# A copy between two DRAM arrays in eight walks: two DMA queues held apart in one address bit at a time

## The chip, the core and the metric

The kernel runs on one core of a Trainium2 chip. The core has 16 DMA engines, and this kernel uses nothing else for its work. The metric is the time of one execution on the device in microseconds. It was 812.63 us before the change (median of three runs, 812.08 to 813.83).

## The reference

```python
def setup_inputs():
    return {
        "x": np.random.randn(8192, 8192).astype(np.float32),
    }

def reference(x: np.ndarray) -> np.ndarray:
    return np.fft.ifftshift(x)
```

For even sizes, ifftshift swaps the halves in both directions: row r of the output is row (r + 4096) mod 8192 of the input, and within a row the two halves of 4,096 columns change places. Nothing is computed. 268.44 MB are read and 268.44 MB written.

## The kernel before

Input and output are arrays in DRAM, and every DMA copies from the one straight into the other. A row of 8,192 floats is 32 KB, a half row 16 KB. A DMA covers half rows only, since the two halves of a row go to different places: `h` is 0 or `hc` (4,096 columns), the half that is written, and the other half of the source row is read.

The helper `copy` (line 26) issues one DMA on a queue. Its access pattern has three dimensions. The first, of 16, steps by one row and is what the 16 DMA engines share out, so each engine gets one row of 16 neighbouring ones. The second, of `per` = 16, steps by 16 rows, so it moves all engines on by 512 KB of addresses (a block of 16 rows). The third is the half row, one contiguous run of 16 KB and one DMA packet. A DMA thus has 256 half rows, 4 MB.

The loop at line 36 takes 1,024 rows at a time, four DMAs of 256 rows for each of two queues: SP's (`nc.sync`, q1) and ACT's (`nc.scalar`, q10). SP's queue writes left halves (`h` = 0) of row groups 0, 1, 2, 3; ACT's queue writes right halves of row groups 2, 3, 0, 1. So the two queues are 512 rows, 16 MB, apart, and in opposite halves, as long as they run side by side. There are 32 DMAs on each queue.

The order in a queue is that of the program. The framework gives each queue four semaphores in turn, so a DMA is issued once the fourth DMA before it in the same queue has landed; up to four are in flight in each. Nothing else orders the work, and no two DMAs touch the same output.

Of the kernel before, what the change touches and what calls it, by code (L numbers as in the profile page):

```python
# [1 line left out]

# [4 lines left out]


ENGINES = 16


@with_exitstack
def kernel(
    ctx: ExitStack,
    tc: tile.TileContext,
    x: bass.AP,
    out: bass.AP,
):
    nc = tc.nc
    R, C = x.shape  # L20
    hr = R // 2
    hc = C // 2
    per = 16
    rows = ENGINES * per

    def copy(queue, row, h, step):

        dims = [[C, ENGINES], [step * C, per], [1, hc]]
        queue.dma_start(
            out=bass.AP(out.tensor, out.offset + row * C + h, dims),  # L30
            in_=bass.AP(x.tensor, x.offset + (row + hr) % R * C + hc - h, dims),
        )

    for first in range(0, R, 4 * rows):
        for n in range(4):
            copy(nc.sync, first + n * rows, 0, ENGINES)
            copy(nc.scalar, first + (n + 2) % 4 * rows, hc, ENGINES)


# [1 line left out]
_INS = ['x']  # L43
_OUTS = [((8192, 8192), 'float32')]


def kernel(**inputs):
    import numpy as _np
    import concourse.bacc as _bacc
    import concourse.tile as _tile  # L50
    from concourse import mybir as _mybir
    from concourse.bass_utils import run_bass_kernel_spmd as _run

    nc = _bacc.Bacc("TRN2", target_bir_lowering=False, num_devices=1)  # L54
    arrays, args = {}, []
    for name in _INS:
        a = _np.ascontiguousarray(inputs[name])
        if a.dtype.kind in "iu":
            a = a.astype(_np.int64)
        arrays[f"in_{name}_dram"] = a  # L60
        args.append(nc.dram_tensor(f"in_{name}_dram", a.shape, _mybir.dt.from_np(a.dtype), kind="ExternalInput").ap())
    for i, (shape, dtype) in enumerate(_OUTS):
        dt = _mybir.dt.from_np(_np.dtype(dtype))
        args.append(nc.dram_tensor(f"out_{i}_dram", shape, dt, kind="ExternalOutput").ap())
    with _tile.TileContext(nc) as tc:
        kernel(tc, *args)
    r = _run(nc, [arrays], core_ids=[0])
    got = tuple(r.results[0][f"out_{i}_dram"] for i in range(len(_OUTS)))
    return got[0]
```

## Time and profile before

| | |
|---|---|
| time, median of 3 runs | 812.63 us (812.08 to 813.83) |
| profiled execution, span | 812.4 us |
| read and written | 268.44 MB each, 661 GB/s together over the span |
| DMA packets | 17,408, of which 1,024 are under 512 B (the completions) |
| issues | 32 on SP's queue, 32 on ACT's, 4,096 KB each, 101.0 us to landing (median) |
| duration of an issue | 571 ns (SP, median), 578 ns (ACT, median) |

The profiled execution lies 0.2 us under the median of the three runs. The profile gives, for each of the two queues, how many packets it had, how many MB they moved, and the time that the packets took as a share of what 16 engines have in the span. The row of DMA digits shows the same share in 40 slices of the span. Compute engines have no work here, and the chain that ended last names none of the copying, since DMA engines are not among its steps; so the queues, the waits of the issuing engines and the single packets are what there is to read. q1 is SP's queue and q10 ACT's.

### The profile page before, as it was taken

To read this page: it belongs to the slowest core of one execution; us is meant where nothing else is said; L and a number is where in the kernel's file an instruction comes from. 1 tells how busy PE (TensorE), PEld (TensorE's weight loads), DVE (VectorE), ACT (ScalarE), POOL (GpSimd) and SP (SyncE) were. 2 spreads that over 40 slices of the span, in tenths; PEclk is the share of its full clock that TensorE was granted. 3 is DMA by queue.
4 is the path that set the end of the run, shared out by engine and by line. 5 is a ranking of instruction groups with operands and counts; after the bars stand their busy time and mean duration, and the time that the engine had idled before them with its cause. 6 is when DMAs were issued, how large, how long until landed. Compare 5 with 4: busy or idle time off the path is not lost. (4 is left out here: it accounts for less than half of the span.)

```text
span 812.4 us, 109 instructions
## 1 busy us (share of the span) xinstructions
POOL 0.2 (0%) x4
## 2 busy tenths in 40 slices
POOL 0000000000000000000000000000000000000000
DMA  9999999999999999999999999999999999999998
GB/s 307 331 331 336 335 331 331 335 325 337 334 332 336 331 333 332 334 339 332 332 334 331 329 331 334 332 328 333 330 334 335 334 328 333 332 331 330 338 331 280
DMA packets 17408, 268.44 MB, mean 330 GB/s; under 512 B 1024, under 2 KB 1024, under 8 KB 1024
## 3 DMA queue, kind: packets, MB, share of 16 engines
q1 hardware_dynamic: 8704, 134.22, 49.7%
q10 hardware_dynamic: 8704, 134.22, 49.5%
HBM read 268.44 MB, written 268.44 MB: 661 GB/s over the span
## 5 line engine op out<-in xcount | busy, mean ns | idle before, releaser
L54 POOL MEMSET const-bfloat16-1.0<- 128x1 bf16 x1 | 0.1, 101 | 0.0
L54 POOL MEMSET const-uint8-127<- 128x1 uint8 x1 | 0.1, 101 | 0.0
L54 POOL MEMSET const-float32-0.0<- 128x1 f32 x1 | 0.1, 98 | 0.2 <-issue 0.2
L54 POOL MEMSET const-float32-1.0<- 128x1 f32 x1 | 0.1, 98 | 0.0
## 6 DMA issues: line engine op xcount, KB each, us to landing
out_dram<-in_x_dram SPq DMA_DIRECT2D x32, 4096.0 KB, 101.0
out_dram<-in_x_dram ACTq DMA_DIRECT2D x32, 4096.0 KB, 101.0
```

Of the source, the lines that this page charges most:

```text
L54: nc = _bacc.Bacc("TRN2", target_bir_lowering=False, num_devices=1)
```

## The change

The rows are divided into eight walks of 1,024 rows (64 blocks of 16 rows). In each walk both queues still copy every half row once between them, one packet for each, over the same 16 engines. What differs is which block each queue is at.

- Walk 0: SP writes blocks 0 to 31, ACT blocks 32 to 63, in opposite halves; then the halves change over. DMAs of 16 blocks, as before.
- Walks 1 to 5 (`apart` with bit 1, 2, 4, 8, 16): SP takes only blocks whose number has that bit clear, ACT only those with the bit set. As a block is 512 KB, the bit is 512 KB, 1 MB, 2 MB, 4 MB or 8 MB of the address. Both queues write the same half, first left, then right. A DMA steps by twice the bit, and so has 32, 16, 8, 4 or 2 blocks.
- Walk 6: bit 1 (512 KB) again, with the queues in opposite halves.
- Walk 7: SP takes blocks 0 to 31 and ACT 32 to 63, in steps of 8 blocks, four to a DMA; the queues are 16 MB apart and alike in all five bits, and in the same half.

There are 84 DMAs on each queue. The waits keep their form: each for the fourth DMA before it in its queue.

```diff
-    per = 16
-    rows = ENGINES * per
 
-    def copy(queue, row, h, step):
-
-        dims = [[C, ENGINES], [step * C, per], [1, hc]]
+    def copy(queue, row, h, by, steps):
+        dims = [[C, ENGINES], [by * ENGINES * C, steps], [1, hc]]
+        dst = out.offset + row * C + h
+        src = x.offset + (row + hr) % R * C + hc - h
         queue.dma_start(
-            out=bass.AP(out.tensor, out.offset + row * C + h, dims),
-            in_=bass.AP(x.tensor, x.offset + (row + hr) % R * C + hc - h, dims),
+            out=bass.AP(out.tensor, dst, dims),
+            in_=bass.AP(x.tensor, src, dims),
         )
 
+    part = 64
 
+    def walk(base, sync, scalar, by, steps, halves):
 
-    for first in range(0, R, 4 * rows):
-        for n in range(4):
-            copy(nc.sync, first + n * rows, 0, ENGINES)
-            copy(nc.scalar, first + (n + 2) % 4 * rows, hc, ENGINES)
+        for hs, ha in halves:
+            for a, b in zip(sync, scalar):
+                copy(nc.sync, (base + a) * ENGINES, hs, by, steps)
+                copy(nc.scalar, (base + b) * ENGINES, ha, by, steps)
+
+    like = ((0, 0), (hc, hc))
+    unlike = ((0, hc), (hc, 0))
+
+    def apart(base, bit, halves):
+        walk(base, range(bit), range(bit, 2 * bit), 2 * bit, part // (2 * bit), halves)
+
+    walk(0, (0, 16), (32, 48), 1, 16, unlike)
+    apart(1 * part, 1, like)
+    apart(2 * part, 2, like)
+    apart(3 * part, 4, like)
+    apart(4 * part, 8, like)
+    apart(5 * part, 16, like)
+    apart(6 * part, 1, unlike)
+    walk(7 * part, range(8), range(32, 40), 8, 4, like)
```

## The prediction

> **What bounds the kernel now.** I read the page first: its DMA row, its queue part and its issue part. Then I asked for the waits of the issuing engines, and last for the queue table of short windows.
>
> ```profile
> span 812.4 us, 109 instructions
> DMA  9999999999999999999999999999999999999998
> GB/s 307 331 331 336 335 331 331 335 325 337 334 332 336 331 333 332 334 339 332 332 334 331 329 331 334 332 328 333 330 334 335 334 328 333 332 331 330 338 331 280
> ...
> q1 hardware_dynamic: 8704, 134.22, 49.7%
> q10 hardware_dynamic: 8704, 134.22, 49.5%
> ...
> out_dram<-in_x_dram SPq DMA_DIRECT2D x32, 4096.0 KB, 101.0
> out_dram<-in_x_dram ACTq DMA_DIRECT2D x32, 4096.0 KB, 101.0
> ```
>
> The 16 DMA engines are busy from end to end; the two queues together fill 99.2% of them. No engine computes anything. Each queue has 8,192 packets of 16 KB and 512 small completion packets of 9 ns (32 DMAs on 16 engines). So one engine carries 1,024 large packets, and 0.992 x 812.4 / 1,024 = 787 ns is the mean of one. The packet records say that a quarter and more of them take exactly 611 ns and one in ten over 1,055 ns: 611 ns is the engine's own pace, the other 176 ns are memory. Packets of one engine follow without a gap, q1 and q10 in turn.
>
> The waits of the queues show that issuing is no bound:
>
> ```profile
> SPq L29 <- DMA out_dram<-in_x_dram: 689.4, 28, 25.3
> SPq L65 <- DMA out_dram<-in_x_dram: 102.2, 2, 79.5
> ```
>
> A DMA waits for the landing of the fourth before it in its own queue; three more are queued on the engines meanwhile, so these 689.4 us cost nothing.
>
> Two neighbouring windows of the queue table (packets, MB, share of 16 engines) show what does vary:
>
> ```profile
> q1 hardware_dynamic: 65, 1.06, 55.6%
> q10 hardware_dynamic: 67, 1.10, 47.9%
> ```
>
> ```profile
> q10 hardware_dynamic: 67, 1.10, 56.7%
> q1 hardware_dynamic: 61, 0.90, 40.9%
> ```
>
> These are 239.3 to 245.5 us and 245.5 to 251.7 us. In the first, a packet of q1 took 0.556 x 16 x 6,200 / 65 = 849 ns and one of q10 709; in the second q1's 55 large packets (0.90 MB) took 738 and q10's 839. Call 16 rows, 512 KB of addresses, a block; each queue is at one block at a time, ACT's queue about 3.3 blocks behind SP's. Summing all packet records by their own block: with the block's 2 MB bit clear 836 ns (q1) and 819 (q10), with it set 740 and 753. So an address bit of a packet's own moves its time by 80 ns. A packet reads and writes at the same offset in the two arrays (but for the half and 128 MB), so this looks like its reads meeting its neighbours' writes; that is my reading, not shown.
>
> **The change part by part.**
>
> *The same bytes, the same packets.* Every half row is still one 16 KB packet, every block is walked once per half, 16 consecutive rows lie on the 16 engines. What a packet's own 2 MB bit costs is therefore paid equally often: 0.
>
> *More DMAs.* 168 instead of 64 (4 + 4, 2 + 2, 4 + 4, 8 + 8, 16 + 16, 32 + 32, 2 + 2, 16 + 16), so 104 more completion packets per engine at 9 ns: +0.9 us on the path. Packets at a DMA's start are not longer than elsewhere (q1 850 ns at block 0 of a DMA, 843 at block 8; q10 787 and 809): 0 besides. Issuing rises from 32 to 84 per queue at 0.571 us (SP) or 0.578 us (ACT), 48 us in all beside 800. The cover is thinnest in the fifth single-bit walk, with DMAs of two blocks. Each new DMA there waits for the fourth before it on its own queue, and all later issues of that queue stand behind it; the other queue is not held. A block of a queue takes 2 x 787 = 1.574 us, so three DMAs of two blocks in flight give 9.4 us. Needed are 1.43 us from issue to first packet (0.73 us to 2.16 at the start), 0.35 us from a last packet to its landing, and the spread of the engines, at most 2.76 us between the first and last of 16 landings of one DMA: 4.5 us. Covered. Were the cover gone in both queues, 32 rounds of up to 4.5 us would cost 144 us.
>
> The Trainium skill ("DMA: Bandwidth & Descriptors", Measured) asks for at least 1 MiB a DMA for 75% of peak, with some 2 us fixed for each; the 512 KB ones break that. Paid once per pair of DMAs it would be 32 x 2 = 64 us, an estimate from that page; the landing rows above, with four in flight, speak against it.
>
> *The distance of the queues.* Before, they are 16 MB apart, less the lag of 3.3 blocks, so lower bits differ or not as the addition carries. I split the packet records by whether the block of the other queue differs in a bit: 512 KB 794 ns (alike 779), 1 MB 789 (786), 2 MB 787 (789), 4 MB 794 (782), 8 MB 796 (785), 16 MB 786 (796). Walking the two lists of blocks with the lag kept gives the share of time apart in each bit, before and after: 0.70 to 0.66, 0.35 to 0.57, 0.83 to 0.50, 0.41 to 0.62, 0.20 to 0.53, 0.90 to 0.58. Products: -0.6, +0.7, +0.7, +2.5, +3.6, +3.2 ns. The last three come largely from the same carries; I count the largest alone: -0.6 + 0.7 + 0.7 + 3.6 = 4.4 ns, x 1,024 = +4.5 us. All counted it is +10 us, none 0. The rows differ by 1 to 3 of their standard errors, so this is weak, but it is all the trace has.
>
> *Like halves, six walks of eight.* Before, the queues are in opposite halves throughout; no row shows the rest. Nearest: moments when over 80% of the running packets belong to one queue, so that nearly all read one half and write the other. These take 774 ns (q1) and 791 (q10), against 791 in even mixtures: like is not worse, and at best 8 ns better, -6 us over 768 packets. Far ends: every like packet in the fast or the slow class of the 2 MB bit, 747 or 828 ns against 787, which is 768 x -40 = -31 us or +31 us. I take 0, being nearest to the mixture rows.
>
> *Strides inside a queue.* An engine's next block is now 1 to 16 MB on, so neighbouring engines, 1 to 2 blocks out of step, are that far apart. It can meet or miss the same reads and writes; bounds as for the halves; I take 0, as each stride meets both classes.
>
> Sum: 812.4 + 0.9 + 4.5 = 817.8 us for the profiled execution; the median of the three runs, 812.63, lies 0.2 higher: **818.0 us**.
>
> **The rivals.**
>
> *Faster: reads and writes kept out of each other's way.* If the 80 ns of the 2 MB bit is a conflict of reads with writes, queues held in like halves keep all reads of both queues in one half. If half of the like packets reach the fast class: 0.5 x 768 x -40 = -15 us, 798 us. For it: the single-queue moments at 774. Against: q10's at 791. It decides once the halves give over 6 ns a packet.
>
> *No change.* Rows 16 apart sit on the same engine, which runs one packet at a time, so the queues never touch the same row position, and their distance does not matter. Only the 0.9 us remain: 813.5 us. For it: differences by bit no larger than 15 ns.
>
> *Slower by the halves.* The opposite: all reads in one half crowd it; half of the like packets in the slow class, +15 us beside the sum: 833 us; all of them, 849.
>
> *Starved queues.* If the engines spread over 9 us in the two-block walk, it costs a few us for each of 32 rounds, 3 x 32: about 910 us. Against: 2.76 us.
>
> *Lock-stepped strides.* If packets 4 to 16 MB apart alias, the walks of the 4 MB and 8 MB bits and the last one (304 us) run at the slowest tenth's 1,055 ns instead of 787: +104 us, 922 us. Against: 16 neighbouring rows are always in flight, 32 KB apart. The Trainium skill ("DMA: Bandwidth & Descriptors", Latency and other measured facts) reports this for copies of 16 KiB rows, 207 GB/s at a pitch of 512 KiB, 164 at 2 MiB, 103 at 4 and 8 MiB; the pitch between engines, which it speaks of, stays 32 KB here, and the queues' 16 MB already run at 330.
>
> **How the numbers follow.** Runs of this kernel tell 0.2% (1.6 us) from no change. Forecast (a little slower, 814.3 to 826) 0.37; slower by the halves 0.15; starved or aliased 0.06; no change 0.13; faster 0.29. Slower 0.58, same 0.13, faster 0.29. The range is to hold 8 in 10: it leaves out the starved and aliased cases, the outer part of the faster case below 798 and of the slower one above 838. The forecast's own range is 814 to 826.
>
> **What would show it.** Eight windows of some 101 us: the first should keep 332 GB/s, the two-block walk should show DMA at 9 throughout, and its issues should land within 13 to 15 us. A walk off by over 3% points to halves (if all like walks go together) or to one bit (if one walk stands out; the seventh, opposite, against the second, like, is the clean pair). Holes in the DMA row of the two-block walk would mean starving. I am wrong if like halves matter as much as the 2 MB bit does.

## The result and the profile after

The changed kernel took 814.69 us (median of 15 runs, 812.76 to 816.6) where the kernel before took 812.08 us (median of 15 runs beside it). The medians lie 2.6 us apart; the ratio worked out from all the runs is 1.0039, with a 95% interval of 1.0026 to 1.0051: slower by about 3.2 us (2.1 to 4.1). The forecast was 818.0 us.

The profiled execution spans 814.2 us, against 812.4 before. A time is not a span: this execution's time was 815.98 us, 1.8 above its span, and every execution with both figures shows 1.7 to 1.8. By that (an estimate) the execution profiled before was one of some 814.2 us, 1.6 above the median rather than 0.2 under it, so the two profiles show 1.8 of the 3.2 us. The page after, in the lines that answer to those shown of before:

```profile
span 814.2 us, 213 instructions
DMA  9999999999999999999999999999999999999998
GB/s 303 332 334 327 335 333 334 334 325 333 332 328 328 325 324 334 331 332 330 328 335 338 332 332 331 332 332 331 338 332 331 341 330 337 335 330 329 323 340 276
...
q1 hardware_dynamic: 9536, 134.22, 50.2%
q10 hardware_dynamic: 9536, 134.22, 48.9%
...
out_dram<-in_x_dram ACTq DMA_DIRECT2D x8, 4096.0 KB, 101.2
out_dram<-in_x_dram SPq DMA_DIRECT2D x8, 4096.0 KB, 103.2
```

The DMA engines are still full from end to end (50.2 + 48.9 = 99.1%), with 1,344 completion packets per queue instead of 512. In the packet records the mean large packet is 786.5 ns in both profiles; the 1.8 us between the spans are 0.9 us of completion packets per engine and 0.9 us more of idle time (7.4 against 6.4 us). So this pair of profiles does not show where the 3.2 us lie. Nothing starved: in the two-block walk the queue table has the DMAs landing as soon as they can with four in flight.

```profile
out_dram<-in_x_dram ACTq DMA_DIRECT2D x32, 512.0 KB, 12.6
out_dram<-in_x_dram SPq DMA_DIRECT2D x32, 512.0 KB, 12.6
```

Four DMAs of two blocks at 1.574 us a block are 12.6 us, a little under the 13 to 15 us forecast. The waits of SP's queue are as harmless as before: 80 waits in 84 issues, the longest as long as one DMA of 32 blocks (32 x 1.574 = 50.4 us).

```profile
SPq L33 <- DMA out_dram<-in_x_dram: 708.1, 80, 50.2
```

The stage table, cut at the eight walks (window, its length, POOL, clock, share of the DMA engines, GB/s), shows how the rate moved from walk to walk:

```profile
3.00:103.00 100.00, 0.00 (x0) 1.00 1.00 334
103.00:204.00 101.00, 0.00 (x0) 1.00 1.00 332
204.00:306.40 102.40, 0.00 (x0) 1.00 0.99 328
306.40:407.70 101.30, 0.00 (x0) 1.00 1.00 331
407.70:508.20 100.50, 0.00 (x0) 1.00 1.00 332
508.20:609.40 101.20, 0.00 (x0) 1.00 1.00 334
609.40:709.30 99.90, 0.00 (x0) 1.00 1.00 335
709.30:809.00 99.70, 0.00 (x0) 1.00 1.00 330
```

The third walk, walk 2 (the 1 MB bit), is the slowest: 328 GB/s, a mean packet of 795.6 ns against 786.5 over all eight, and the only one under a full DMA share. In the packet records, cut at these windows, 0.9 us of time per engine lay idle there, against 0.3 us at most in the other walks. One profile tells 1% in a walk from chance only just (the mean of a walk's packets has a standard error of some 4.5 ns), so the candidates were made into kernels of their own that walk all rows in one way.

### The profile page after: what moved, and what is told of

It reads as the page before. It is cut to its first block, busy times and chain, and to the rows that moved or that the text cites. A ratio compares the mean times of both kernels' runs of the same rounds, so it can differ in the third digit from the quotient of the medians.

```text
span 814.2 us, 213 instructions
## 1 busy us (share of the span) xinstructions
POOL 0.2 (0%) x4
## 3 DMA queue, kind: packets, MB, share of 16 engines
q1 hardware_dynamic: 9536, 134.22, 50.2%
q10 hardware_dynamic: 9536, 134.22, 48.9%
```

## The experiments

The experiments ran on three chips, each kernel beside the kernel before on the same chip. Chip A ran the first four (kernel before: 823.28 us), chip B the next four (822.23 us), chip C those of the last part, "What about the step" (813.19 us). So the ratios are what to read, and a ratio from one chip set against one from another carries the difference of the chips as well; the absolute times in the expectations are meant for 812 us. The theories: that the 3.2 us are the price of more DMAs, of where the queues stand to each other (halves, or a bit of the address), or of how each queue steps through memory.

### More DMAs, in the old order

```diff
-    per = 16
-    rows = ENGINES * per
+    per = 2
+    rows = ENGINES * 16
...
-            copy(nc.sync, first + n * rows, 0, ENGINES)
-            copy(nc.scalar, first + (n + 2) % 4 * rows, hc, ENGINES)
+            for k in range(0, rows, 2 * ENGINES):
+                copy(nc.sync, first + n * rows + k, 0, ENGINES)
+                copy(nc.scalar, first + (n + 2) % 4 * rows + k, hc, ENGINES)
```

> The blocks of before in the order of before, cut into DMAs of two blocks: 512 DMAs for 64, and nothing else changed. Theory count (the whole 3.2 us of the change are its 104 more DMAs, 31 ns each): 448 more cost 13.8 us, 826 us. Theory distance (a DMA costs its 9 ns completion packets alone, the rest of the 3.2 us is where the queues stand): +4.0 us, 816 us. Starving would show as holes in the DMA row and far more than 826.

Measured: ratio 1.0011 (0.9996 to 1.0027), 823.59 us. 448 more DMAs cost 0.9 us (-0.3 to +2.2), so 31 ns a DMA are ruled out; even the 4.0 us of the completion packets alone lie outside the interval. One thing moved along with it: in the packet records the one queue led the other by 0.9 us instead of 5.3. The completion packets did take their time (512 per engine at 9 ns, 4.6 us), while the mean large packet was 790.2 ns, against 795.8 in the next kernel on the same chip. So a gain from the shorter lead may hide a part, and the count may still be worth its 0.9 us of completion packets in the changed kernel, where the lead stayed at some 5 us. The issue lines of this kernel:

```profile
out_dram<-in_x_dram ACTq DMA_DIRECT2D x256, 512.0 KB, 12.7
out_dram<-in_x_dram SPq DMA_DIRECT2D x256, 512.0 KB, 12.7
```

The Trainium skill ("DMA: Bandwidth & Descriptors", Measured) wants at least 1 MiB a DMA, for 75% of peak. The page gives that for loads into on-chip memory issued by GpSimd (and the prediction's 2 us, under another heading, for DMAs of GpSimd too); here the two queues are SP's and ACT's, and the copy goes from DRAM to DRAM. These DMAs are half of that size, in all of the kernel, and with four in flight in each queue the kernel takes 0.1% longer, which is not told from nothing.

### Like halves

```diff
-        for n in range(4):
-            copy(nc.sync, first + n * rows, 0, ENGINES)
-            copy(nc.scalar, first + (n + 2) % 4 * rows, hc, ENGINES)
+        for h in (0, hc):
+            for n in range(2):
+                copy(nc.sync, first + n * rows, h, ENGINES)
+                copy(nc.scalar, first + (n + 2) * rows, h, ENGINES)
```

> Before with both queues in the same half, still 16 MB apart, 64 DMAs of 16 blocks. If halves do not matter (taken at 0 in the prediction): within 0.2% of before, 811 to 814 us. If like halves cost: all 1,024 packets of an engine are like here, so a cost seen over 768 of them in the change is 4/3 as large here; with 2.3 us of the 3.2 from halves, 815 us or more. If like halves relieve reads and writes: under 810 us.

Measured: 1.0008 (0.999 to 1.0025). Halves do not matter within 0.25%, at steps of 512 KB.

### The seventh and the third walk for all rows

The seventh (512 KB bit, opposite halves):

```diff
-    for first in range(0, R, 4 * rows):
-        for n in range(4):
-            copy(nc.sync, first + n * rows, 0, ENGINES)
-            copy(nc.scalar, first + (n + 2) % 4 * rows, hc, ENGINES)
+    for first in range(0, R, 2 * rows):
+        for h in (0, hc):
+            copy(nc.sync, first, h, 2 * ENGINES)
+            copy(nc.scalar, first + ENGINES, hc - h, 2 * ENGINES)
```

> All rows walked as the seventh walk was: the queues apart in the 512 KB bit, opposite halves, 64 DMAs of 16 blocks. The walk's mean packet was 778.6 ns in the profile of the change against 786.5 over all. Theory distance: that holds, 1,024 x 8 ns = 8 us, 804 us. Theory count (distance costs nothing and the walks differ by chance): 811 to 813.5 us.

Measured: 1.0019 (1.0006 to 1.0032). The 8 us of gain that the profile's fastest walk promised are not there. Chance is the likely reason of its 778.6 ns: in the second profile of the changed kernel (below) this walk has 792.8 ns against 794.6 over all. The interval lies above 1, so this kernel, whose queues step by 1 MB, is a little slower than before.

The third (1 MB bit, same half):

```diff
-        for n in range(4):
-            copy(nc.sync, first + n * rows, 0, ENGINES)
-            copy(nc.scalar, first + (n + 2) % 4 * rows, hc, ENGINES)
+        for h in (0, hc):
+            for a in range(2):
+                copy(nc.sync, first + a * ENGINES, h, 4 * ENGINES)
+                copy(nc.scalar, first + (2 + a) * ENGINES, h, 4 * ENGINES)
```

> All rows walked as the third walk was: the queues apart in the 1 MB bit, same half, 64 DMAs of 16 blocks. The walk's mean packet was 795.6 ns, the slowest of the eight, and it had 0.94 us of idle time per engine, the most of those before the end. Theory distance: 1,024 x 9 ns = 9 us more and 8 x 0.7 us of idle, up to 826 us. Theory count: 811 to 813.5 us.

Measured: 1.0156 (1.013 to 1.0181), 835.81 us. This one is real, and larger than the 9 ns of one profile: 12.8 us for all rows, 1.6 us for the eighth of the rows in the changed kernel.

### The step against the distance

That walk does two things: it keeps the queues apart in the 1 MB bit, and it moves each queue on by four blocks, 2 MB, at a time. Two kernels take them one by one. The step alone, with the queues 32 MB apart:

```diff
-    for first in range(0, R, 4 * rows):
-        for n in range(4):
-            copy(nc.sync, first + n * rows, 0, ENGINES)
-            copy(nc.scalar, first + (n + 2) % 4 * rows, hc, ENGINES)
+    for first in range(0, R, 8 * rows):
+        for h in (0, hc):
+            for a in range(4):
+                copy(nc.sync, first + a * ENGINES, h, 4 * ENGINES)
+                copy(nc.scalar, first + 4 * rows + a * ENGINES, h, 4 * ENGINES)
```

> The 1 MB walk cost 1.56% when all rows went by it. It has two parts: the queues stand apart in the 1 MB bit, and each queue goes on by 2 MB from block to block. Here the second alone: steps of 2 MB in each queue, same half, the queues 32 MB apart and alike in the bits 512 KB to 16 MB when level; 64 DMAs of 16 blocks. If the stride costs: a ratio of about 1.016 to before. If the distance in the 1 MB bit costs: 1.000 to 1.002, as like halves alone gave 1.0008.

The distance alone, two neighbouring blocks to a DMA:

```diff
-    per = 16
-    rows = ENGINES * per
+    per = 2
+    rows = ENGINES * 16
...
-        for n in range(4):
-            copy(nc.sync, first + n * rows, 0, ENGINES)
-            copy(nc.scalar, first + (n + 2) % 4 * rows, hc, ENGINES)
+        for h in (0, hc):
+            for k in range(0, 4 * rows, 4 * ENGINES):
+                copy(nc.sync, first + k, h, ENGINES)
+                copy(nc.scalar, first + k + 2 * ENGINES, h, ENGINES)
```

> The other part alone: SP's queue takes blocks 0, 1, 4, 5, 8, 9 ..., ACT's 2, 3, 6, 7, 10, 11 ..., same half, in DMAs of two neighbouring blocks (512 DMAs, which cost 1.0011 in the order of before). The queues are apart in the 1 MB bit throughout, and no queue steps by 2 MB. If the distance costs: about 1.016. If the stride costs: 1.000 to 1.003.

Measured: the step alone 1.0142 (1.0117 to 1.0168), 833.26 us; the distance alone 1.0 (0.9987 to 1.0012), 822.51 us. The step carries the cost, and the queues may stand as they like in that bit. The pairs kernel has short DMAs and a short lead (1.0 us); the kernel of short DMAs in the old order, which has both as well, gave 1.0011, so the distance adds nothing to that. The pages of the two, the step first, show the engines full in both, at different rates:

```profile
span 831.6 us, 109 instructions
DMA packets 17408, 268.44 MB, mean 323 GB/s; under 512 B 1024, under 2 KB 1024, under 8 KB 1024
q10 hardware_dynamic: 8704, 134.22, 50.1%
q1 hardware_dynamic: 8704, 134.22, 48.8%
```

```profile
span 819.5 us, 557 instructions
DMA packets 24580, 268.50 MB, mean 328 GB/s; under 512 B 8192, under 2 KB 8192, under 8 KB 8192
q1 hardware_dynamic: 12288, 134.23, 49.9%
q10 hardware_dynamic: 12288, 134.23, 49.5%
```

Both fill the engines to about 99%; in the packet records the mean large packet is 802.5 ns with the step and 790.7 without, and 1,024 x 11.8 ns = 12.1 us is the difference of the spans, 12.1. Two smaller terms cancel: the engines are idle for 4.1 us more with the step (9.3 against 5.2 us), and the short DMAs have 4.0 us more of completion packets. So it is mainly the packets that last longer.

### The changed kernel again, and the last walk for all rows

The changed kernel as it is, on chip B:

> The changed kernel itself beside the others, since another chip gave before 823 us where the first gave 812. If the 0.39% belongs to the walks and not to the first chip: 1.003 to 1.005. Of it the 1 MB walk gives 1.56/8 = 0.20.

Measured: 1.0044 (1.0031 to 1.0057). The last walk (same half, steps of 4 MB, four blocks to a DMA):

```diff
-    per = 16
-    rows = ENGINES * per
+    per = 4
+    rows = ENGINES * 16
...
-        for n in range(4):
-            copy(nc.sync, first + n * rows, 0, ENGINES)
-            copy(nc.scalar, first + (n + 2) % 4 * rows, hc, ENGINES)
+        for h in (0, hc):
+            for a in range(8):
+                copy(nc.sync, first + a * ENGINES, h, 8 * ENGINES)
+                copy(nc.scalar, first + 2 * rows + a * ENGINES, h, 8 * ENGINES)
```

> All rows walked as the last walk was: same half, 16 MB apart, alike in the bits 512 KB to 8 MB when level, steps of 4 MB in a queue, 256 DMAs of four blocks. Its mean packet in the profile of the change was 791.2 ns against 786.5 over all. If that is the walk and not chance: 1.006. If strides are what costs and grow with the step: over 1.016. If only the 1 MB bit or the 2 MB stride costs: 1.000 to 1.002.

Measured: 1.0054 (1.0034 to 1.0073). So the 0.39% is the kernel's and not the chip's, and steps of 4 MB cost too, less than those of 2 MB. A part of the 0.54% can be the 192 more DMAs of that kernel: 0.05% by the 0.11% for 448 above, 0.21% by 9 ns each. On this chip the mean large packet goes with the ratios: 790.7 ns in the pairs kernel, 794.6 in the changed one, 800.5 with steps of 4 MB, 802.5 with steps of 2 MB. The stage table of the second profile of the changed kernel has its two lowest rates in walks 2 and 3, with steps of 2 and 4 MB (here walks 2 to 4); walk 7, also with steps of 4 MB, has 329, like walk 0:

```profile
206.00:309.00 103.00, 0.00 (x0) 1.00 0.99 324
309.00:412.00 103.00, 0.00 (x0) 1.00 0.99 325
412.00:513.50 101.50, 0.00 (x0) 1.00 1.00 330
```

### What about the step

A step of 2.5 MB instead of 2 (five blocks), for 480 of the 512 blocks:

```diff
-    for first in range(0, R, 4 * rows):
-        for n in range(4):
-            copy(nc.sync, first + n * rows, 0, ENGINES)
-            copy(nc.scalar, first + (n + 2) % 4 * rows, hc, ENGINES)
+    for top in (0, hr):
+        for first in range(top, top + 15 * rows, 5 * rows):
+            other = top + (first - top + 5 * rows) % (15 * rows)
+            for a in range(5):
+                copy(nc.sync, first + a * ENGINES, 0, 5 * ENGINES)
+                copy(nc.scalar, other + a * ENGINES, hc, 5 * ENGINES)
+        copy(nc.sync, top + 15 * rows, 0, ENGINES)
+        copy(nc.scalar, top + 15 * rows, hc, ENGINES)
```

> Steps of five blocks, 2.5 MB, in each queue, for 480 of 512 blocks (32 blocks go by single blocks), opposite halves as before, 64 DMAs of 16 blocks. Theory alias (a step of a bare power of two from 2 MB on brings packets that run together onto the same part of memory): the step also moves the 512 KB bit, so nothing is lost, 1.000 to 1.002. Theory distance of the step (a far step costs whatever its bits are): 480/512 of the 1.42% of the 2 MB step, 1.013.

Measured: 1.0009 (0.9991 to 1.0027). A farther step does not cost as such, so the distance to the next packet is not what counts; that a bare power of two is what counts is the likely reading. It is not shown clean: the two kernels with 2 MB steps ran on chips A and B and had both queues in the same half, this one ran on chip C with opposite halves, and it is the only step tried from 2 MB on that is no power of two.

The 2 MB step on one side only. These two kernels leave out the right order of the rows: as many bytes are read and written, but blocks land in other places than the reference puts them. The loop is that of the step kernel; the copy takes one block number for the far side and one for the near side (shown for the writes; the reads' kernel has the two exchanged):

```diff
+        far, near = a * ENGINES, a * rows
+        to, come = first + far, (first + near + hr) % R
...
-            out=bass.AP(out.tensor, out.offset + row * C + h, dims),
-            in_=bass.AP(x.tensor, x.offset + (row + hr) % R * C + hc - h, dims),
+            out=bass.AP(out.tensor, out.offset + to * C + h, [[C, ENGINES], [4 * ENGINES * C, per], [1, hc]]),
+            in_=bass.AP(x.tensor, x.offset + come * C + hc - h, [[C, ENGINES], [1 * ENGINES * C, per], [1, hc]]),
```

> The writes of the 2 MB stride kernel with reads block by block: only the write side steps by 2 MB; blocks land in another order than the reference has them, with the same bytes read and written. Theory writes: 1.014, and the reads' counterpart 1.000. Theory reads: 1.000. Theory both sides alike: 1.007 in each. Theory meeting (reads of one block meet writes of another only if both sides step alike): 1.000 in each.

> The counterpart: only the read side steps by 2 MB, the writes go block by block; blocks land in another order than the reference has them. Theory reads: 1.014. Theory writes: 1.000. Theory both sides alike: 1.007. Theory meeting: 1.000.

Measured: 1.0036 (1.0015 to 1.0057) for the writes, 1.0021 (1.0003 to 1.004) for the reads. Neither side carries the 1.42%, and together, 0.57% (at most 0.97% by the ends of their intervals, against 1.17% at least), they are well short of it. That no theory had foreseen: a good part of the cost appears only when both sides step by 2 MB. Two things differ besides: the 1.42% comes from chip B and these two from chip C, where steps of 2 MB on both sides were not run; and a packet here reads and writes at different offsets of the two arrays, where in the other kernels they are alike but for the half and the 128 MB. It fits reads of one packet meeting writes of another in memory, but no run shows that they meet, or where.

Steps of 8 MB, with long DMAs:

```diff
-    for first in range(0, R, 4 * rows):
-        for n in range(4):
-            copy(nc.sync, first + n * rows, 0, ENGINES)
-            copy(nc.scalar, first + (n + 2) % 4 * rows, hc, ENGINES)
+    for first in (0, hr):
+        for h in (0, hc):
+            for a in range(8):
+                copy(nc.sync, first + a * ENGINES, h, 16 * ENGINES)
+                copy(nc.scalar, first + (8 + a) * ENGINES, h, 16 * ENGINES)
```

> All rows walked as the fifth walk was, with longer DMAs: steps of 8 MB in each queue, queues apart in the 4 MB bit, same half, 64 DMAs of 16 blocks. So far 1 MB steps cost 0.19%, 2 MB 1.42 to 1.56%, 4 MB 0.54%. Theory alias with a cost that falls again above 2 MB, as those numbers have it: 1.001 to 1.005, and then the eight walks add up to the 0.44% (with the sixth, whose steps are 16 MB every other time, alike). Theory that every step from 2 MB on costs about alike, with the 4 MB run low for its short DMAs: 1.010 to 1.016; then the walks add up to more than 0.44%.

Measured: 1.0099 (1.0073 to 1.0124): clear of the first theory, and at the lower end of the second. The cost has not gone at 8 MB. By step, then: 512 KB is the kernel before; 1 MB 0.19%; 2 MB 1.42 and 1.56%; 2.5 MB 0.09%, not told from none; 4 MB 0.54% (in chains of four blocks); 8 MB 0.99%.

Taken together, an eighth each: walks 1 and 6 at 0.19 (walk 1 was not run in its like halves), walk 2 at 1.56, walks 3 and 7 at 0.54, walk 4 at 0.99, walk 0 at 0, make 4.01 / 8 = 0.50% without walk 5, whose steps are 16 MB every other time and which was not run alone. Measured were 0.39% (0.26 to 0.51) and 0.44% (0.31 to 0.57). So the steps can account for the whole of it, though adding up eighths from kernels on three chips is an estimate, and the 0.9 us of completion packets (0.11%) may take a part. What does not fit is walk 4: it ran at 332 and 330 GB/s in the two profiles of the changed kernel, no less than the others; with it at 0 the sum is 3.02 / 8 = 0.38%. It has chains of only four blocks there and 16 in the kernel of its own; whether that is the reason stays open. No kernel of these beats the one before.

## Why the prediction was right, and where it was not

The direction and the size came out: slower, by 3.2 us where 5.4 over the median were forecast, inside the forecast's own range of 814 to 826. The route was only partly right, and that the sum came near was luck.

*The same bytes, the same packets: 0.* Right: the mean large packet is 786.5 ns in both profiles. The 2 MB bit still splits the packets; sorted by it, those of walk 0 took 796 ns with the bit clear and 736 with it set in SP's queue, 858 and 747 in ACT's. Walk 3 sorts the two queues by just this bit, and the queue table of its window (306.4 to 407.7 us) has them apart:

```profile
q1 hardware_dynamic: 1151, 16.76, 54.2%
q10 hardware_dynamic: 1149, 16.73, 45.7%
```

SP's 1,023 large packets took 0.542 x 16 x 101,300 / 1,023 = 859 ns and ACT's 1,021 took 725, while the rate stayed at 331 GB/s. Not all of these 134 ns are the bit's: in walk 2 (204 to 306.4 us) each queue goes over both values of the bit equally often, and the queues are apart all the same, by the same working 829 and 755 ns:

```profile
q1 hardware_dynamic: 1090, 16.81, 51.9%
q10 hardware_dynamic: 1088, 16.78, 47.2%
```

Why one queue's packets last longer there stays open. The prediction's split of a packet into 611 ns of the engine and the rest of memory is a reading too: what the records show is that 27 to 33% of the large packets take exactly 611 ns in every profile, while the mean goes from 786.5 to 804.0.

*More DMAs: +0.9 us.* Issue and landing were hidden as argued. The residue is between 0.2 us (104 of them by the 0.9 us that 448 cost) and the 0.9 us of their completion packets; no run parts the two. The spread of the engines grew from 2.76 us to 4.1 at most, so 1.43 + 0.35 + 4.1 = 5.9 us were needed of the 9.4.

*The distance of the queues: +4.5 us.* This step failed. It was read from differences of 1 to 3 standard errors, split by bits that the lag's carries tie together, and it assumed that SP's queue leads by 3.3 blocks. In both profiles of the changed kernel ACT's queue led, by some 4.9 us. Where a run isolates a distance, the 1 MB bit, it costs 0.0%, and the kernels with the 2 MB step cost about alike with the queues 1 MB apart (1.56%) and 32 MB apart (1.42%). The 8 MB bit, which had the +3.6 ns, was isolated by no run, and neither was the lead; so a small part of the term may be real.

*Like halves: 0.* Right, 1.0008. The two rivals that were built on the halves, *Faster* and *Slower by the halves*, fall with it.

*Strides inside a queue: 0.* This is where most of the 3.2 us are, by the sum of eighths above. The step was named, and bounded as widely as the halves, but costed at nothing because "each stride meets both classes" of the 2 MB bit. That argument holds for single packets and misses what runs together: at a step of 2 MB an engine that is one block ahead and one behind it are a bare 2 MB apart, on both the read and the write side. That this is how the cost arises is a reading; that a step of 2 MB costs, 1.42% over all rows, where the distance does not, is shown. The sum was near by luck: a +4.5 that the runs do not bear out stood in for a missing +3.

*The rivals.* Starving was rightly put far off. "Lock-stepped strides" came nearest to the place, but looked for it at 4 to 16 MB and so left out walk 2, whose 2 MB step costs the most. Its price was far too high: 104 us for three walks, where whole kernels of two of them gave 0.99% and 0.54%, some 1 us for an eighth of the rows at most. The rule of the Trainium skill that stood beside it ("DMA: Bandwidth & Descriptors", Latency and other measured facts) has 164 GB/s of 207 left at a pitch of 2 MiB and half at 4 MiB, with a padded pitch as the cure. That rule speaks of the pitch between streams that run side by side, which stays 32 KB in all kernels here, so no run tries it. For steps in time the direction is alike (2 MB costs, 2.5 MB does not; a pitch padded by a few KB was not tried), and the size is far smaller: 1.4% at 2 MB, 0.5% at 4 MB.

## What to carry to other kernels

When a copy keeps its DMA engines full, look at the step from one packet to the next within a queue before the distance between queues: steps of 2, 4 and 8 MB cost 0.5 to 1.6% here over steps of 512 KB, while 2.5 MB cost nothing that can be measured. A term that could be 31 us either way and is taken at 0 by an argument of symmetry needs a run of its own. The size of a DMA hardly matters as long as those that wait in flight cover the issue and the landing: 3 x 3.15 us against 5.9 us here.

## What the runs showed of the hardware that was not expected

The same kernel differs by 1.4% from chip to chip (812.08 and 823.28 us), so only ratios from one chip compare cleanly.

The sign of the 2 MB bit is no property of the address in the array. On chip B walk 3 of the very same kernel had the classes the other way round (309 to 412 us):

```profile
q10 hardware_dynamic: 1151, 16.76, 51.7%
q1 hardware_dynamic: 1149, 16.73, 47.6%
```

Here SP's packets, with the bit clear, took 768 ns and ACT's 833. It is no property of the chip either: on chip B too, the kernel with the 2 MB step alone has the packets with the bit clear slower (815 against 768 ns in SP's queue, 845 against 782 in ACT's). Where the two arrays lie in memory may decide it; the profile doesn't tell their addresses. One queue's loss was the other's gain each time (means of 792 and 800 ns for the two together, 786.5 and 794.6 over all walks), so the 80 ns that the prediction saw look like a matter of who waits more than of how much is moved.

The queue whose first packet comes first leads to the end: SP's by 5.3 us in the kernel before, ACT's by 3.9 to 5.5 us, walk by walk, in both profiles of the changed kernel; with DMAs of two blocks throughout the lead is about 1 us.
